# A two-layer decoder trunk: down projections whose sums are collected by adding transfers, with five pairs per group by seven block products

## The chip, the cores and the metric

The kernel runs on one core of one Trainium2 chip. The time is the device time of one execution in microseconds (us). A core has a matrix engine (TensorE, here PE, with its weight loads as PEld), a vector engine (VectorE, DVE), a scalar engine (ScalarE, ACT), a general engine (GpSimd, POOL) and a sync engine (SyncE, SP), which here only issues transfers. Each engine works through its own list in order and waits on semaphores of the others. Transfers (DMA) run beside them and raise a semaphore when they land.

## The reference, cut to what matters

The model has two layers over 256 tokens of width 2048. Layer A is a gated spatial mixer, layer B a latent attention; both have an attention into 256 memory tokens beside them, and each is followed by a gated ConvFFN:

```python
def conv_ffn(h, w_up, cw, cb, w_down):          # D_FF = 5632, width 3
    a = h @ w_up                                 # 2048 -> 11264
    ap = jnp.pad(a, ((0, 0), (CONV_W - 1, 0), (0, 0)))
    c = sum(ap[:, k:k + S] * cw[k] for k in range(CONV_W)) + cb
    gate, val = c[..., :D_FF], c[..., D_FF:]
    return (jax.nn.silu(gate) * val) @ w_down    # 5632 -> 2048

x = x + conv_ffn(rmsnorm(x, g_ffn[l]), w_ffn_up[l], conv_w[l], conv_b[l], w_ffn_down[l])
```

Everything is float32. The change is in the last product, `@ w_down`.

## The kernel before

Every float32 weight tile is split into a high part (`whi`, an ACT copy) and a low part (`wlo`, a DVE subtraction, raw minus high), and each product is made of three matmuls: high by high, high by low, low by high. A weight tile thus goes through four steps: SP issues its load into a `raw` buffer (four buffers of 128x1024, 512 KB each), ACT makes `whi`, DVE makes `wlo` (four buffers of each), TensorE multiplies.

`ffn` works through the hidden width in three groups of 4, 4 and 3 times 512 (`FF_GROUPS`). For each group the up projection is computed by `gemm_fm`, the convolution by `conv` on DVE and ACT, and the result is kept in `h`, sixteen blocks of 128 hidden units for the groups of four. Then this group's part of the down projection follows. For the first two groups of each layer this is `gemm_seven`, the function that the change rewrites; there are four such calls in the kernel, called groups below. The third group of a layer goes through `gemm_fm` or `gemm_tm`.

`gemm_seven` treats `h` as eight pairs of blocks and the output as two halves of 1024 columns, so it has sixteen steps, half 0 and then half 1, pairs 0 to 7 in each. A step is the product of a 2x2 arrangement: two blocks of tokens, two blocks of hidden units (a pair), two blocks of 512 output columns. A plain pair takes eight block products of three matmuls each, 24 matmuls, added up in four banks (`out`). The pairs in `SEVEN` take seven block products, 21 matmuls, as in Strassen's scheme in a form with few sums: three of the seven use differences of weight blocks (`differences`, on DVE, into `gate` buffers, split like any weight), four use sums of blocks of `h` (`block_sums`, computed in the up projection). Four results go to banks of their own (`side`) and are combined at the end of a half (`combined`). A seven pair thus needs four `whi` and four `wlo`, a plain pair two of each.

The steps are a software pipeline. In iteration i the program issues the first differences of step i + 2, then the split parts of step i + 1 (`prepare`), then the second differences of step i + 2, and then the matmuls of step i (`products`). The order on PE, ACT, DVE and SP is held as written (`manual_schedule`); elsewhere a scheduler sets it. A pair's raw data is loaded where it is first asked for (`load`, from `differences` or `prepare`).

The results of a half are added into `total` (layer A) or `xt` (layer B) in on-chip memory: `collected` adds the four banks, `combined` writes or adds the block products' sums, all of it by DVE (`add`, line 297). The small sums are spread over the following steps, three per step.

Of the kernel before, what the change touches and what calls it, by code (L numbers as in the profile page):

```python
# [8 lines left out]
F32 = mybir.dt.float32  # L9
# [7 lines left out]
P = 128  # L17
# [17 lines left out]
WARM = 7  # L35
SEVEN = (3, 5)

# [65 lines left out]
class Kernel:  # L103
# [189 lines left out]

    def gemm_seven(self, dn, n, h, s7, total, fresh, pool):
        nc = self.nc
        sub = lambda o, a, b: nc.vector.tensor_tensor(o, a, b, ALU.subtract)
        add = lambda o, a, b: nc.vector.tensor_tensor(o, a, b, ALU.add)
        ET = mybir.EngineType
        steps = [(half, m) for half in range(2) for m in range(n)]
        src = lambda i, c: self.rows(dn, (2 * steps[i][0] + c) * 512, 512)(2 * steps[i][1], 2)  # L300
        seven = lambda i: i < len(steps) and steps[i][1] in s7
        raws, early, ready, later = {}, {}, {}, []
        out, side = {}, {}

        def load(i):
            raws[i] = [self.raw_load(src(i, c)) for c in range(2)]

        def differences(i, part):
            if part == 0:
                load(i)  # L310
                early[i] = [self.tmp(pool, [P, 4, S], "gate", 2).rearrange("p a s -> p (a s)") for _ in range(2)]
            (b11, b21), (b12, b22) = ((raw[:, :512], raw[:, 512:]) for raw in raws[i])
            (t1, t2), (t3, t4) = ((t[:, :512], t[:, 512:]) for t in early[i])
            if part == 0:
                sub(t1, b12, b11)
                sub(t3, b22, b12)
            else:
                sub(t2, b22, t1)
                sub(t4, b21, t2)

        def prepare(i):
            if i not in raws:
                load(i)
            one, two = raws.pop(i)
            if seven(i):
                ta, tb = early.pop(i)
                ready[i] = [self.weight_parts(w) for w in (one, two[:, 512:], ta, tb)]
            else:
                ready[i] = [self.weight_parts(w) for w in (one, two)]

# [3 lines left out]
        def products(i):  # L334
            half, m = steps[i]
            parts = ready.pop(i)
            pick = lambda w, j: (w[0][:, j, :], w[1][:, j, :])
            if m == 0:
                for key in ((0, 0), (0, 1), (1, 0), (1, 1)):
                    out[key] = self.psum()  # L340
            if not seven(i):
                for c in range(2):
                    for tb in range(2):
                        for j in range(2):
                            first, last = m + j == 0, m == n - 1 and j == 1
                            self.three(out[tb, c], block(2 * m + j, tb), pick(parts[c], j), first, last)
                return
            first, last = m == min(s7), m == max(s7)
# [4 lines left out]
            one, b22, ta, tb = parts  # L353
            self.three(side[1], block(2 * m, 0), pick(one, 0), first, last)
            self.three(out[0, 0], block(2 * m + 1, 0), pick(one, 1))
            self.three(out[0, 1], s[3], pick(b22, 0))
            self.three(side[5], s[0], pick(ta, 0), first, last)
            self.three(side[6], s[1], pick(ta, 1), first, last)
            self.three(side[7], s[2], pick(tb, 0), first, last)
            self.three(out[1, 0], block(2 * m + 1, 1), pick(tb, 1))  # L360
            if last:
                later.extend(combined(half, dict(side)))
# [5 lines left out]
        def combined(half, p):  # L368
# [23 lines left out]
            if not fresh:  # L392
                todo += [lambda k=k, at=at: add(to[at], to[at], t[k]) for k, at in ((1, (0, 0)), (5, (0, 1)), (7, (1, 0)), (0, (1, 1)))]
            return todo

        def collected(half, accs):
            return [lambda at=at, acc=acc: add(place(half, *at), place(half, *at), acc) for at, acc in accs.items()]

        with self.tc.manual_schedule(engines={ET.PE, ET.Activation, ET.DVE, ET.SP}):
            prepare(0)  # L400
            for i in range(len(steps)):
                if seven(i + 2):
                    differences(i + 2, 0)
# [8 lines left out]
                if steps[i][1] == n - 1:  # L412
                    later.extend(collected(steps[i][0], dict(out)))
            for f in later:
                f()
# [74 lines left out]
    def masks(self):  # L490
        nc, cp = self.nc, self.cp
        self.ident = cp.tile([P, P], F32, name="ident")
# [29 lines left out]
    def rope_tables(self, la):  # L522
# [30 lines left out]
        nc.vector.tensor_tensor(k, k, k, ALU.mult)  # L553
        self.cosT = cp.tile([P, S], F32, name="cosT")
        self.sinT = cp.tile([P, S], F32, name="sinT")
        nc.vector.tensor_scalar(self.cosT, k, -2.0, 1.0, ALU.mult, ALU.add)
# [226 lines left out]
    def next_operand(self, j, gain):  # L783
# [6 lines left out]
        self.square_add(self.ssum, x, j == 0, self.cp)  # L790

# [13 lines left out]

    def ffn(self, l, sums, total, fresh, after=None, hooks={}, tokens=None):
        nc, t = self.nc, self.t
# [4 lines left out]
        with self.tc.tile_pool(name=self.uid("ff"), bufs=1) as fp:  # L812
            g0 = 0
            for part, ng in enumerate(FF_GROUPS):
# [41 lines left out]
                if not last:  # L856
                    self.gemm_seven(dn, 2 * ng, h, s7, total, fresh and part == 0, fp)
                    g0 += ng
                    continue
# [104 lines left out]
    def layer_b(self):  # L964
# [9 lines left out]
        with tc.tile_pool(name="lb", bufs=1) as lb:  # L974
# [8 lines left out]
            def latent(name):  # L983
# [3 lines left out]
                def evict(b, acc):  # L987
                    self.scaled(lat[:, b : b + 2, :], acc, rb)
                    self.square_add(sums, lat[:, b : b + 2, :], b == 0, self.cp)

# [182 lines left out]
    def first_ffn(self):  # L1173
        nc, tc = self.nc, self.tc
        with tc.tile_pool(name="sums", bufs=1) as sp:
# [4 lines left out]
            def turn(a, i):  # L1180
                small[a, i] = self.tmp(sp, [P, 1024], "s7" if a == 0 else "square", len(SEVEN) if a == 0 else 2)
                src = total[:, a, 1024 * i : 1024 * (i + 1)]
# [21 lines left out]
            }  # L1204
            self.ffn(0, sp, total, True, after=lambda j: self.next_operand(j, None), hooks=hooks)

    def run(self):
# [10 lines left out]
        with tc.tile_pool(name="fin", bufs=1) as fin, tc.tile_pool(name="sums", bufs=1) as sums_pool:  # L1218
# [11 lines left out]
            def gains():  # L1230
                gb.append(slot()[:, :D])
                nc.sync.dma_start(out=gb[0], in_=t["g_final"].rearrange("(o d) -> o d", o=1).to_broadcast([P, D]))

# [123 lines left out]
```

## Time and profile before

| | |
|---|---|
| median of 3 runs | 2037.37 us (2033.04 to 2039.13) |
| the profiled execution | 2035.25 us, span 2033.5 us |
| PE, DVE, ACT, POOL busy | 2020.3, 1493.2, 1080.7, 95.1 us |
| granted TensorE clock | 0.999 |
| the first `gemm_seven`, 520.6 to 605.0 us | PE busy 83.64 of 84.4 us, DVE 69.35, ACT 43.00; DMA share 0.61 |
| the third, 1481 to 1570 us | PE busy 86.96 of 89 us; DMA share 0.60 |

In the profile, a group row reads: line, engine, operation, output tile and input tiles, shape and count, then the busy time and the mean duration in ns of one, then the idle time of the engine ahead of them and what ended it. The durations of matmuls are from start to end and overlap; TensorE's rate is read from the distance of two starts. A waits row reads: who waited for whom, then the total in us, how often, and the longest. Transfers show the median time from issue to landing. Tile names stand without their numbers, so that `raw7` may appear as `raw`.

### The profile page before, as it was taken

The numbers are of one execution on the slowest core, as the hardware profiler recorded it, in microseconds if no ns is written. First come the engines' busy times: TensorE is split into PE (matmuls) and PEld (weight loads), VectorE is DVE, ScalarE is ACT, GpSimd is POOL, SyncE is SP. The second block draws the span as 40 slices with busy tenths as digits, with TensorE's granted clock in tenths as the row PEclk, the third lists the DMA queues.
The fourth block names the chain that finished last, engine by engine and source line by source line (L and its number), as shares of the span: only waits on it lengthen the run. The fifth ranks groups of instructions, "written<-read, shape, count | busy, mean of one in ns | idle before, by whom it ended". The sixth has DMA issues, their size and how long they took to land.

```text
span 2033.5 us, 37724 instructions
## 1 busy us (share of the span) xinstructions
PE 2020.3 (99%) x15394; PEld 1923.9 (95%) x15394; DVE 1493.2 (73%) x2064; ACT 1080.7 (53%) x1424; POOL 95.1 (5%) x131
## 2 busy tenths in 40 slices
PE   9999999999999999999999999999999999999998
PEld 8989999999889998899999999999988999889997
DVE  6866667767776777877789886777678667786675
ACT  6754644555545555445546674455544555544543
POOL 0000013000000000000052002200000000000000
PEclk9999999999999999999999999999999999999999
DMA  8675855666566665688665565578756666566654
GB/s 312 186 236 176 199 179 186 206 190 192 185 213 190 195 196 180 213 214 214 190 195 185 172 151 166 192 209 214 222 186 199 195 201 188 183 204 195 199 185 154
DMA packets 254013, 398.86 MB, mean 196 GB/s; under 512 B 65040, under 2 KB 71824, under 8 KB 253712
## 3 DMA queue, kind: packets, MB, share of 16 engines
q1 hardware_dynamic: 253264, 395.80, 64.7%
q8 instruction: 120, 1.97, 0.4%
q10 hardware_dynamic: 576, 0.66, 0.1%
q14 instruction: 53, 0.43, 0.1%
HBM read 388.01 MB, written 2.10 MB: 192 GB/s over the span
## 4 chain that ended last, share of the span: by engine, by line
PE 94%; DVE 3%; DMA 2%; issue 1%; ACT 1%; ACTq 0%; POOLq 0%; POOL 0%; DVEq 0%
PE ps L180 23%; PE ps L181 23%; PE ps L183 23%; PE ps L291 4%; PE ps L292 4%; PE ps L290 4%; PE ps L211 3%; PE ps L212 3%; PE ps L213 3%; DMA raw<-in_w_ffn_down 1%; DVE wlo L270 1%; DVE c L828 0%; ACT whi L269 0%; PE ps L714 0%; PE ps L767 0%
## 5 line engine op out<-in xcount | busy, mean ns | idle before, releaser
L144 DVE TENSOR_TENSOR wlo<-raw,whi 128x1024 fp32r<-128x1024 f32 (+1 forms) x544 | 664.3, 1238 | 396.2 <-issue 254.0
L143 ACT ACTIVATE whi<-raw 128x1024 fp32r<-128x1024 f32 (+1 forms) x544 | 569.4, 1054 | 574.1 <-PE ps L181 435.6
L180 PE MATMUL ps<-xhl,whi 128*128 128x256 f32 x3264 | 750.6, 276 | 0.0
L181 PE MATMUL ps<-xhl,whi 128*128 128x256 f32 x3264 | 750.2, 276 | 0.0
L180 PEld LDWEIGHTS ps<-xhl,whi 128*128 128x128 f32 x3264 | 612.6, 188 | 0.2
L181 PEld LDWEIGHTS ps<-xhl,whi 128*128 128x128 f32 x3264 | 612.6, 188 | 0.2
L183 PE MATMUL ps<-xhl,wlo 128*128 128x256 f32 x3264 | 403.2, 276 | 0.0
L183 PEld LDWEIGHTS ps<-xhl,wlo 128*128 128x128 f32 x3264 | 385.2, 188 | 0.0
L269 ACT ACTIVATE whi<-raw 128x1024 fp32r<-128x1024 f32 (+1 forms) x128 | 126.0, 1004 | 113.8 <-DMA raw<-in_w_ffn_down 45.8
L270 DVE TENSOR_TENSOR wlo<-raw,whi 128x1024 fp32r<-128x1024 f32 (+1 forms) x128 | 144.8, 1155 | 48.3 <-ACT whi L269 22.2
L291 PE MATMUL ps<-wlo,h 128*128 128x512 f32 x432 | 168.7, 391 | 2.5 <-DVE wlo L270 2.5
L290 PE MATMUL ps<-whi,h 128*128 128x512 f32 x432 | 168.4, 390 | 1.3 <-ACT whi L269 1.3
L292 PE MATMUL ps<-whi,h 128*128 128x512 f32 x432 | 168.2, 389 | 0.0
L828 DVE SCALAR_TENSOR_TENSOR c<-a,cT,c 128x255 f32<-128x255 f32 (+1 forms) x352 | 145.9, 477 | 0.0
L825 ACT ACTIVATE c<-a,cT 128x256 f32<-128x256 f32 x176 | 91.6, 591 | 77.4 <-DVE a L419 77.4
L180 PE MATMUL ps<-mainhl,whi 128*128 128x256 f32 x512 | 118.5, 278 | 0.0
L181 PE MATMUL ps<-mainhl,whi 128*128 128x256 f32 x512 | 118.0, 277 | 0.0
L291 PEld LDWEIGHTS ps<-wlo,h 128*128 128x128 f32 x432 | 81.1, 188 | 21.2 <-DVE wlo L270 4.4
L290 PEld LDWEIGHTS ps<-whi,h 128*128 128x128 f32 x432 | 81.1, 188 | 18.6 <-ACT whi L269 1.9
L292 PEld LDWEIGHTS ps<-whi,h 128*128 128x128 f32 x432 | 81.1, 188 | 16.8
L180 PEld LDWEIGHTS ps<-mainhl,whi 128*128 128x128 f32 x512 | 96.0, 188 | 0.1
L181 PEld LDWEIGHTS ps<-mainhl,whi 128*128 128x128 f32 x512 | 96.0, 188 | 0.1
(325 smaller groups left out, 2389.6 us busy)
## 6 DMA issues: line engine op xcount, KB each, us to landing
raw<-in_w_ffn_up SPq DMA_DIRECT2D x352, 512.0 KB, 4.2
raw<-in_w_ffn_down SPq DMA_DIRECT2D x176, 512.0 KB, 4.8
raw<-in_w_out SPq DMA_DIRECT2D x64, 512.0 KB, 4.9
raw<-in_w_in_a SPq DMA_DIRECT2D x56, 512.0 KB, 4.5
raw<-in_w_mem_kv SPq DMA_DIRECT2D x31, 512.0 KB, 5.3
raw<-in_w_in_b SPq DMA_DIRECT2D x16, 512.0 KB, 3.9
raw<-in_w_uq SPq DMA_DIRECT2D x12, 384.0 KB, 3.4
raw<-in_w_kv_a SPq DMA_DIRECT2D x8, 512.0 KB, 3.7
```

The source lines that it names most:

```text
L143: nc.scalar.activation(hi[:, :n], raw[:, :n], AF.Copy)
L144: nc.vector.tensor_tensor(lo[:, :n], raw[:, :n], hi[:, :n].bitcast(F32), ALU.subtract)
L180: mm(acc, wh, x[:, :S], start=first, stop=False)
L181: mm(acc, wh, x[:, S:], start=False, stop=False)
L183: mm(acc, wl, x[:, :S], start=False, stop=last)
L269: nc.scalar.activation(hi, raw, AF.Copy)
L270: nc.vector.tensor_tensor(lo, raw, hi.bitcast(F32), ALU.subtract)
L290: mm(acc, xh, wh, start=start, stop=False)
L291: mm(acc, xh, wl, start=False, stop=False)
L292: mm(acc, xl, wh, start=False, stop=stop)
L825: nc.scalar.activation(c[:, i, :], a[:, i, :], AF.Identity, scale=w(2), bias=w(3))
L828: nc.vector.scalar_tensor_tensor(o, a[:, i, : S - 2 + j], w(j), o, ALU.mult, ALU.add)
```

## The change

- The pairs by seven block products are now 4 and 6 in half 0 and 2, 4 and 6 in half 1, where they were 3 and 5 in both. In half 0 the pairs run in the order 0, 1, 2, 4, 3, 6, 5, 7 (`PASSES`). By position in the sixteen steps, counted from 0, the seven pairs stand at 3, 5, 10, 12 and 14; before they stood at 3, 5, 11 and 13.
- A seven pair's raw weights, 1 MB, go to a tile of their own, `raw7`, with one buffer, in three transfers: a row of 128x1024 and two of 128x512. Plain pairs keep the four `raw` buffers. Room for `raw7` is made by moving constants to other pools, and in layer B it is the second half of the gain vector's tile.
- All loads are asked for in the order of the steps, two steps ahead.
- The first two differences are now one instruction of 128x1024.
- Sums that were added to `total` by DVE are now added by transfers on POOL's queue with an adding operation (`collect`). A bank's result is first copied by ACT to a `c` buffer (three buffers, shared with the convolution), since the transfer starts from there. The first group of layer A still writes the block products' sums straight to `total`.
- Four instead of three of the small steps run per step.

```diff
-SEVEN = (3, 5)
+SEVEN = (2, 4, 6)
+PASSES = (((0, 1, 2, 4, 3, 6, 5, 7), (4, 6)), ((0, 1, 2, 3, 4, 5, 6, 7), (2, 4, 6)))
...
         def load(i):
-            raws[i] = [self.raw_load(src(i, c)) for c in range(2)]
+            half, m = steps[i]
+            if not seven(i):
+                blocks[i] = [self.raw_load(src(i, c)) for c in range(2)]
+                return
+            raw = blocks[i] = raw7()
+            row = lambda j: self.rows(dn, half * 1024, 1024)(2 * m + j, 1).rearrange("p k (c n) -> p (k c) n", c=2)
+            nc.sync.dma_start(out=raw[:, 0:2, :], in_=row(0))
+            for c in range(2):
+                nc.sync.dma_start(out=raw[:, 3 - c, :], in_=row(1)[:, c, :])
 
         def differences(i, part):
+            raw = blocks[i]
             if part == 0:
-                load(i)
...
+                sub(early[i][0], raw[:, 1:3, :], raw[:, 0:2, :])
+                return
+            t13, t24 = early[i]
+            sub(t24[:, 0, :], raw[:, 2, :], t13[:, 0, :])
+            sub(t24[:, 1, :], raw[:, 3, :], t24[:, 0, :])
...
             if not fresh:
-                todo += [lambda k=k, at=at: add(to[at], to[at], t[k]) for k, at in ((1, (0, 0)), (5, (0, 1)), (7, (1, 0)), (0, (1, 1)))]
+                todo += [lambda k=k, at=at: collect(to[at], t[k]) for k, at in ((1, (0, 0)), (5, (0, 1)), (7, (1, 0)), (0, (1, 1)))]
             return todo
 
+        def collect(to, x):
+            nc.gpsimd.dma_start(out=to, in_=x, accum_op=ALU.add)
+
         def collected(half, accs):
-            return [lambda at=at, acc=acc: add(place(half, *at), place(half, *at), acc) for at, acc in accs.items()]
+            def one(at, acc):
+                c = self.tmp(pool, [P, 2, S], "c", 3).rearrange("p a s -> p (a s)")
+                nc.scalar.activation(c, acc, AF.Copy)
+                collect(place(half, *at), c)
+
+            return [lambda at=at, acc=acc: one(at, acc) for at, acc in accs.items()]
 
         with self.tc.manual_schedule(engines={ET.PE, ET.Activation, ET.DVE, ET.SP}):
+            load(0)
+            load(1)
             prepare(0)
             for i in range(len(steps)):
+                if i + 2 < len(steps):
+                    load(i + 2)
                 if seven(i + 2):
                     differences(i + 2, 0)
                 if i + 1 < len(steps):
                     prepare(i + 1)
                 if seven(i + 2):
                     differences(i + 2, 1)
-                now, later[:] = later[:3], later[3:]
+                now, later[:] = later[:4], later[4:]
                 products(i)
...
-            self.ffn(0, sp, total, True, after=lambda j: self.next_operand(j, None), hooks=hooks)
+            self.ffn(0, sp, total, True, lambda: self.tmp(sp, [P, 4, 512], "raw7", 1), after=lambda j: self.next_operand(j, None), hooks=hooks)
...
-            self.ffn(1, sums_pool, xt, False, hooks=turns, tokens=tokens)
+            self.ffn(1, sums_pool, xt, False, lambda: gb[0][:, D:].rearrange("p (a n) -> p a n", a=4), hooks=turns, tokens=tokens)
```

Three places where the order of instructions changes. First SP's queue, at the loads of the first `gemm_seven`; a row gives the buffer's number, the weight matrix, the shape and the semaphores waited for. Before, from position 2 and 3 on (the seven pair's loads, 757 and 758, stand ahead of position 2's, 761 and 762):

```order
L262 DMA raw_757_6086<-in_w_ffn_down 128x2x512 [waits DMAHW0_49,DVE_49]
L262 DMA raw_758_6088<-in_w_ffn_down 128x2x512 [waits DMAHW1_49,DVE_49]
L262 DMA raw_761_6094<-in_w_ffn_down 128x2x512 [waits DMAHW2_49,DVE_49]
L262 DMA raw_762_6096<-in_w_ffn_down 128x2x512 [waits DMAHW3_49,DVE_49]
L262 DMA raw_775_6172<-in_w_ffn_down 128x2x512 [waits DMAHW6_49,DVE_49]
L262 DMA raw_776_6174<-in_w_ffn_down 128x2x512 [waits DMAHW7_49,DVE_49,Activation_49]
L262 DMA raw_779_6180<-in_w_ffn_down 128x2x512 [waits DMAHW4_49,DVE_49]
L262 DMA raw_780_6182<-in_w_ffn_down 128x2x512 [waits DMAHW5_49,DVE_49]
```

Now the same place:

```order
L263 DMA raw_751_6058<-in_w_ffn_down 128x2x512 [waits DMAHW0_49,DVE_49]
L263 DMA raw_752_6060<-in_w_ffn_down 128x2x512 [waits DMAHW1_49,DVE_49]
L316 DMA raw7_761_6098<-in_w_ffn_down 128x1024 [waits PE_49,Pool_49]
L318 DMA raw7_761_6098<-in_w_ffn_down 128x512 x2
L263 DMA raw_768_6139<-in_w_ffn_down 128x2x512 [waits DMAHW2_49,DVE_49]
L263 DMA raw_769_6141<-in_w_ffn_down 128x2x512 [waits DMAHW3_49,DVE_49]
L316 DMA raw7_778_6183<-in_w_ffn_down 128x1024 [waits DMAHW6_49,DMAHW0_49,DMAHW7_49,DVE_49,Activation_49]
L318 DMA raw7_778_6183<-in_w_ffn_down 128x512 [waits DMAHW4_49]
L318 DMA raw7_778_6183<-in_w_ffn_down 128x512 [waits DMAHW5_49]
L263 DMA raw_789_6225<-in_w_ffn_down 128x2x512
L263 DMA raw_790_6227<-in_w_ffn_down 128x2x512
```

Position 4's load (768, 769) has moved ahead of position 5's (778), and position 5's now waits for DVE's and ACT's reads of position 3 out of the one `raw7` buffer; position 6's load (789, 790) stands right behind it.

Second DVE, at the same place. Now:

```order
L297 TENSOR_TENSOR gate_763_6103<-raw7_761_6098,gate_763_6103 128x512 [waits DMAHW7_49,DVE_49]
L271 TENSOR_TENSOR wlo_771_6144<-raw7_761_6098,whi_770_6143 128x512 [waits PE_49]
L271 TENSOR_TENSOR wlo_773_6148<-raw7_761_6098,whi_772_6147 128x1024 [waits PE_49]
L271 TENSOR_TENSOR wlo_775_6152<-gate_762_6102,whi_774_6151 128x1024 [waits Activation_49]
L271 TENSOR_TENSOR wlo_777_6156<-gate_763_6103,whi_776_6155 128x1024 [waits Activation_49]
L297 TENSOR_TENSOR gate_779_6187<-raw7_778_6183 128x1024 [waits DMAHW5_49,DMAHW3_49,DVE_49]
L271 TENSOR_TENSOR wlo_782_6191<-raw_768_6139,whi_781_6190 128x1024 [waits DMAHW1_49,Activation_49]
L271 TENSOR_TENSOR wlo_784_6195<-raw_769_6141,whi_783_6194 128x1024 [waits DMAHW2_49,Activation_49]
L297 TENSOR_TENSOR gate_780_6188<-raw7_778_6183,gate_779_6187 128x512 [waits DVE_49]
L297 TENSOR_TENSOR gate_780_6188<-raw7_778_6183,gate_780_6188 128x512 [waits DMAHW4_49,DVE_49]
L271 TENSOR_TENSOR wlo_792_6230<-raw7_778_6183,whi_791_6229 128x512 [waits Activation_49]
L271 TENSOR_TENSOR wlo_794_6234<-raw7_778_6183,whi_793_6233 128x1024 [waits Activation_49]
```

Position 5's first difference (`gate_779`) stands ahead of position 4's low parts (`wlo_782`, `wlo_784`), as it did before; but its load is now the one that starts after `wlo_773`, the last read of position 3's `raw7`.

Third ACT, where half 0's results are collected during position 8. Now:

```order
L270 ACTIVATE whi_823_6391<-raw_813_6346 128x1024 [waits DMAHW5_49,DVE_49,PE_49]
L408 ACTIVATE c_829_6425<-ps_757_6070 128x512
L408 ACTIVATE c_830_6428<-ps_758_6071 128x512
L408 ACTIVATE c_831_6431<-ps_759_6072 128x512
L408 ACTIVATE c_832_6434<-ps_760_6073 128x512 [waits DMASW0_49,Activation_49]
L270 ACTIVATE whi_835_6441<-raw7_818_6380 128x512 [waits DMAHW6_49,DVE_49,PE_49]
L270 ACTIVATE whi_837_6445<-raw7_818_6380 128x1024 [waits DMAHW0_49,DMAHW7_49,DVE_49,PE_49]
```

The four copies are new on ACT (before, ACT went from one `whi` to the next here); the fourth waits for `DMASW0`, the landing of the first copy's transfer on POOL's queue, and position 10's `whi` stand behind it.

More of the change, by code (lines that the diff above doesn't have):

```diff
@@ L298, in gemm_seven @@
         ET = mybir.EngineType
-        steps = [(half, m) for half in range(2) for m in range(n)]
+        steps = [(half, m) for half, (order, _) in enumerate(passes) for m in order]
         src = lambda i, c: self.rows(dn, (2 * steps[i][0] + c) * 512, 512)(2 * steps[i][1], 2)
-        seven = lambda i: i < len(steps) and steps[i][1] in s7
-        raws, early, ready, later = {}, {}, {}, []
+        seven = lambda i: i < len(steps) and steps[i][1] in passes[steps[i][0]][1]
+        begins = [passes[half][0][0] == m for half, m in steps]
@@ L303, in gemm_seven @@
+        ends = [passes[half][0][-1] == m for half, m in steps]
+        heavy = [[i for i in range(len(steps)) if steps[i][0] == half and seven(i)] for half in range(len(passes))]
+        blocks, early, ready, later = {}, {}, {}, []
         out, side = {}, {}
         def load(i):
-            raws[i] = [self.raw_load(src(i, c)) for c in range(2)]
+            half, m = steps[i]
[7 more added lines that the diff above has]
+                nc.sync.dma_start(out=raw[:, 3 - c, :], in_=row(1)[:, c, :])
@@ L308, in differences @@
         def differences(i, part):
+            raw = blocks[i]
             if part == 0:
-                load(i)
[L311 to L319, printed above, removed]
+                early[i] = [self.tmp(pool, [P, 4, S], "gate", 2).rearrange("p (a b) s -> p a (b s)", a=2) for _ in range(2)]
+                sub(early[i][0], raw[:, 1:3, :], raw[:, 0:2, :])
+                return
@@ L321, in prepare @@
+            t13, t24 = early[i]
+            sub(t24[:, 0, :], raw[:, 2, :], t13[:, 0, :])
+            sub(t24[:, 1, :], raw[:, 3, :], t24[:, 0, :])
         def prepare(i):
-            if i not in raws:
-                load(i)
-            one, two = raws.pop(i)
+            raws = blocks.pop(i)
             if seven(i):
[L326 to L329, printed above, removed]
+                flat = lambda x: x.rearrange("p a s -> p (a s)")
+                raws = [raws[:, 0, :], flat(raws[:, 2:4, :])] + [flat(t) for t in early.pop(i)]
@@ L344, in products @@
                         for j in range(2):
-                            first, last = m + j == 0, m == n - 1 and j == 1
+                            first, last = begins[i] and j == 0, ends[i] and j == 1
                             self.three(out[tb, c], block(2 * m + j, tb), pick(parts[c], j), first, last)
                 return
-            first, last = m == min(s7), m == max(s7)
+            first, last = i == heavy[half][0], i == heavy[half][-1]
             if first:
@@ L352, in products @@
             s = [(s7[m][:, 0, j, :], s7[m][:, 1, j, :]) for j in range(4)]
[L353 to L360, printed above, removed]
+            b11, b2, t13, t24 = parts
+            self.three(side[1], block(2 * m, 0), pick(b11, 0), first, last)
+            self.three(out[0, 0], block(2 * m + 1, 0), pick(b2, 1))
+            self.three(out[0, 1], s[3], pick(b2, 0))
+            self.three(side[5], s[0], pick(t13, 0), first, last)
+            self.three(side[7], s[2], pick(t13, 1), first, last)
+            self.three(side[6], s[1], pick(t24, 0), first, last)
+            self.three(out[1, 0], block(2 * m + 1, 1), pick(t24, 1))
             if last:
@@ L803, in w_out, with ffn @@
             group(g)
-    def ffn(self, l, sums, total, fresh, after=None, hooks={}, tokens=None):
+    def ffn(self, l, sums, total, fresh, raw7, after=None, hooks={}, tokens=None):
         nc, t = self.nc, self.t
@@ L856, in ffn @@
                 if not last:
-                    self.gemm_seven(dn, 2 * ng, h, s7, total, fresh and part == 0, fp)
+                    self.gemm_seven(dn, PASSES, h, s7, total, fresh and part == 0, fp, raw7)
                     g0 += ng
@@ L1180, in turn @@
             def turn(a, i):
[L1181 removed]
+                if a == 0:
+                    small[a, i] = self.tmp(sp, [P, 1024], "s7", len(SEVEN))
+                elif i == 0:
+                    both = self.tmp(sp, [P, 2, 1024], "raw7", 1)
+                    small[1, 0], small[1, 1] = both[:, 0, :], both[:, 1, :]
                 src = total[:, a, 1024 * i : 1024 * (i + 1)]
```

21 lines of the change are left out of this document (11 added, 10 removed).

## The prediction

> **What bounds the kernel now.** I read the page first: busy shares and the chain that ended last.
>
> ```profile
> span 2033.5 us, 37724 instructions
> PE 2020.3 (99%) x15394; PEld 1923.9 (95%) x15394; DVE 1493.2 (73%) x2064; ACT 1080.7 (53%) x1424; POOL 95.1 (5%) x131
> PE ps L180 23%; PE ps L181 23%; PE ps L183 23%; PE ps L291 4%; PE ps L292 4%; PE ps L290 4%; PE ps L211 3%; PE ps L212 3%; PE ps L213 3%; DMA raw<-in_w_ffn_down 1%; DVE wlo L270 1%; DVE c L828 0%; ACT whi L269 0%; PE ps L714 0%; PE ps L767 0%
> ```
>
> TensorE sets the end; the stages to change are lines 290 to 292. Next, what TensorE waited for there, from the waits of PE, and then the chain through the start of a down projection, where such a wait arises (start, duration, piece).
>
> ```profile
> PE ps L291 <- DVE wlo L270: 2.5, 4, 0.8
> PE ps L290 <- ACT whi L269: 1.3, 1, 1.3
> ```
> ```profile
> 534.05 1.15 DVE wlo L270
> 535.21 5.35 DMA raw<-in_w_ffn_down
> 540.66 1.07 ACT whi L269
> 541.76 1.23 DVE wlo L270
> 543.04 0.50 PE ps L291
> 543.76 0.23 PE ps L290
> ...
> 544.44 0.23 PE ps L290
> ```
>
> The same chain of the whole span has such a load at the other three groups too:
>
> ```profile
> 794.79 4.95 DMA raw<-in_w_ffn_down
> ...
> 1496.48 6.99 DMA raw<-in_w_ffn_down
> ...
> 1757.95 5.28 DMA raw<-in_w_ffn_down
> ```
>
> Only 2.5 + 1.3 = 3.8 us of TensorE waiting belongs to these stages, so nothing large can be won. But the chain shows how thin the cover is: a `raw` buffer is read for the last time, only then is the next load issued, 5 to 7 us later it lands, is split by ACT and DVE, and TensorE has run dry. This happens once in each of the four groups, at the fifth pair. Three matmuls take 544.44 - 543.76 = 0.68 us, so one is 0.227; a plain pair of 24 takes 5.45, a seven pair of 21 takes 4.77, both together 10.2 us.
>
> **The matmuls.** A seven pair is one computed by seven block products instead of eight. There are 20 of them instead of 16 (five per group), and each new one saves one block product of three matmuls: 4 x 3 x 0.227 = **2.7 us off**. Pair 4's old wait goes as well, since its load now stands ahead of the next seven pair's: **3.8 us off**.
>
> **The raw buffer.** A seven pair's 1 MB now goes to `raw7`, which exists once, instead of to two of the four `raw` buffers. Durations by shape, over the whole run:
>
> ```profile
> L270 DVE TENSOR_TENSOR wlo<-raw,whi 128x1024 fp32r<-128x1024 f32 x112 | 135.2, 1222 | 48.3 <-ACT whi L269 22.2 <-issue 18.5 <-PE ps L183 6.2
> L269 ACT ACTIVATE whi<-gate 128x1024 fp32r<-128x1024 f32 x32 | 34.0, 1062 | 56.4 <-PE ps L292 52.6 <-DVE wlo L270 3.8
> L296 DVE TENSOR_TENSOR gate<-raw,gate 128x512 f32<-128x512 f32 x32 | 22.0, 688 | 0.4
> L270 DVE TENSOR_TENSOR wlo<-raw,whi 128x512 fp32r<-128x512 f32 x16 | 10.9, 684 | 0.0
> L269 ACT ACTIVATE whi<-raw 128x512 fp32r<-128x512 f32 x16 | 10.0, 625 | 9.4 <-PE ps L292 6.2 <-ACT whi L269 3.2
> L284 DVE TENSOR_TENSOR s<-c,s 128x512 fp32r<-128x512 f32 x8 | 5.6, 694 | 5.8 <-ACT s L283 5.8
> L281 DVE TENSOR_TENSOR c<-hv 128x128 f32<-128x128 f32 x16 | 3.9, 283 | 0.0
> L375 ACT ACTIVATE a<-ps 128x512 f32<-128x512 f32 x6 | 3.5, 580 | 0.0
> ```
> ```profile
> 533.96 1.83 DVE L270 TENSOR_TENSOR wlo<-raw,whi 128x1024 fp32r<-128x1024 f32 x2
> ```
>
> By the order on DVE, what lies between the landing of one seven pair and the last read of its buffer is: the first difference (128x1024, 1.22), the two low parts of the pair before it (2 x 1.22), two differences of 512 (2 x 0.69), and the low parts of its own two raw pieces (0.68 + 1.22): 6.9 us, and since a 1.22 and a 0.68 end in 1.83 in the row above, each start overlaps by 0.08: **6.5 us**. Then the next load may start. Behind that load wait DVE's next difference, behind this on the same engine the plain pair's low parts (already landed), and behind them TensorE.
>
> How long does 1 MB take? Rows for it:
>
> ```profile
> 541.98 2.53 ACT L269 ACTIVATE whi<-raw 128x1024 fp32r<-128x1024 f32 x3 [0.26 <-DMA raw<-in_w_ffn_down]
> ```
> ```profile
> raw<-in_w_ffn_down SPq DMA_DIRECT2D x176, 512.0 KB, 4.8
> xt<-slot SPq DMA_DIRECT2D x16, 128.0 KB, 5.6
> turned<-square SPq DMA_DIRECT2D x16, 64.0 KB, 6.1
> slot<-in_g_final SPq DMA_DIRECT2D x1, 1024.0 KB, 4.9
> out_y<-xt SPq DMA_DIRECT2D x3, 256.0 KB, 2.9
> ...
> turned<-in_w_sp SPq DMA_DIRECT2D x1, 768.0 KB, 9.4
> ```
>
> In the chain the first half of a pair lands 5.35, 4.95, 6.99 and 5.28 us after its issue (mean 5.6), the second half 541.98 - 540.66 = 1.3 later: 6.9 for 1 MB. The gain vector's 1 MB took 4.9, the lower bound. In the new order SP issues the following 1 MB right behind; shared fully it would add 2 x 1.3: 9.6, the upper bound. I take 7.3, close to the pair, which is the same tensor on the same queue.
>
> Three loads per group must wait for the one buffer (positions counted from 0):
> - Position 5 after 3. Before, the last raw read of position 3 ended at 533.96 + 1.83 = 535.8. The sums of the new sixth pair now stand ahead of it on DVE (4 x 0.28 + 0.69 = 1.8): 537.6. Plus 7.3, plus difference and low part (2.3): 547.2. TensorE wants it at 543.04 less its wait, about 542.0: **5.2** (2.8 to 7.5).
> - Position 12 after 10. The buffer's last reads need a free `whi`, which comes when TensorE ends position 8 (the 52.6 us in the row of L269 are such waits): 1.06 + 1.22 later the load starts, 7.3 + 2.3 later the low part of position 11 is there: 11.9 against 10.4 (10.2 and one matmul): **1.5** (0 to 3.8).
> - Position 14 after 12, now in a closed ring: 6.5 + 7.3 = 13.8 against 10.2: **3.6** (1.2 to 5.9).
>
> Sum 10.3 per group, **41 us** (16 to 69).
>
> **The adding transfers.** 32 results go from a matmul bank to `c` by an ACT copy (0.58 each, L375) and from there by a POOL-queue transfer; 24 more, in the three groups that are not the first, leave `a` and `hv`. DVE loses 56 adds, which is worth nothing, since DVE is not the bound. But `c` has three buffers and each half has four results: the fourth copy waits on ACT until the first transfer has landed, X after its issue, and behind it on ACT stand the next `whi`. No row shows an adding transfer. The nearest are 2.9 (256 KB to HBM), 5.6 and 6.1 (small pieces moved inside the on-chip memory); the slowest of all is 9.4. I take X = 5.6, since it too stays on the chip, and keep 2.9 and 9.4 as the ends.
> In mid-group the first copy ends 0.58 into position 8, and the fourth at X + 1.16; then 0.63 + 1.06 + 1.22 until the buffer of position 10 is free: X + 4.1 instead of 5.45 + 2.3 = 7.75. X - 3.7 = 1.9, four times: 7.6. At a group's end the fourth `whi` of the next projection, wanted after 5.45 + 1.8 = 7.25 (48 and 16 matmuls of half the length), stands behind the fourth copy. In the first group it comes at X + 0.58 + 0.58 + 1.06 = 7.8: 0.6 late. In the three groups that add to earlier totals the first copy's transfer also waits for the block product's on the same quarter, issued 0.58 into the last pair: that lands at X + 0.58 - 5.45 = 0.7, the copy's at 6.3, `whi` at 6.3 + 0.58 + 1.06 = 8.0: 0.8 late, three times. Together **11 us** (0, or with 9.4: 4 x 5.7 + 4.4 + 3 x 8.4 = 52).
>
> [...]
>
> **Sum.** -2.7 - 3.8 + 41 + 11 = +46 us on the profiled execution's 2035.25 (span 2033.5 and 1.75 around it): 2081. The median of the runs shown, 2037.37, is 2 above it: **2083**. The added sums of pairs 2 and 4 in each up projection lie in DVE's idle time there (busy 73% by the page; uncovered, 4 x 1.8 = 7 us) and the moved constants cost nothing.
>
> **Rivals.**
> 1. Quick loads: 1 MB in 4.9 as the gain vector, and transfers in 2.9. 16 + 0 - 6.5: +9.5, 2047 on the median. For it: rows of 4 KB in one piece. Against it: four measured pairs. 0.13. [...]
> 2. Slow adding transfers, X = 9.4: 41 + 52 - 6.5 = +86, 2124. For it: small pieces already take 6.1, and these queue behind one another on POOL. Against it: each is only 256 KB in rows of 2 KB. 0.14.
> 3. Faster: the two old waits go and no new one comes. This needs 1 MB within 10.2 - 6.5 = 3.7 us in the ring, and within 542.0 - 537.6 - 2.3 = 2.1 at position 5. Then 6.5 us come off: 2031. For it: plain pairs are now loaded a step earlier, so the queue is emptier when the buffer comes free. Against it: even 512 KB has a median of 4.8. 0.03.
> 4. No change: 1 MB in 3.7, so that the ring costs nothing and position 5 costs 4 x 1.6 = 6.4, which takes the 6.5 back: 2037. The same row speaks against it. 0.05.
>
> My forecast has 0.65. This measurement tells about 0.3% (6 us) from no change. Slower 0.90 (a part of rival 1 falls within 6 us), same 0.07, faster 0.03. The range 2045 to 2135 reaches from quick loads to slow transfers; the forecast's own is 2055 to 2115.
>
> **What would show it.** Right: DVE's difference line (now 297) waits for DMA tens of us in total; TensorE's line 292 waits for `wlo` at the pair ahead of a seven pair, three times per group, and the chain there reads load, difference, low part, matmul; the fourth ACT copy (line 408) waits for a POOL transfer. Wrong: if the 1 MB lands under 5 us, or the difference finds its data waiting, the 41 falls; if line 408 never waits, the 11 falls.

## The result, and the profile after

| | before | after |
|---|---|---|
| median | 2035.8 us | 2101.74 us (2099.7 to 2109.52) |
| ratio, 95% interval | | 1.033 (1.0299 to 1.0362) |
| the profiled execution, its span | 2035.25, 2033.5 us | 2102.6, 2100.9 us |
| granted TensorE clock | 0.999 | 0.987 |

The change makes the kernel 66 us slower. The page of the kernel after, with the rows that answer to those of before (the chain by engine, the matmuls on a low part):

```profile
span 2100.9 us, 37918 instructions
PE 2044.0 (97%) x15382; PEld 1936.2 (92%) x15382; DVE 1482.1 (71%) x2032; ACT 1109.8 (53%) x1468; POOL 144.2 (7%) x187
PE 86%; DMA 6%; DVE 4%; issue 2%; SPq 1%; ACT 1%; DVEq 0%; POOLq 0%; POOL 0%; ACTq 0%
L292 PE MATMUL ps<-wlo,h 128*128 128x512 f32 x412 | 171.2, 416 | 47.1 <-DVE wlo L271 47.1
```

And its waits (who for whom, total us, times, longest):

```profile
PE ps L292 <- DVE wlo L271: 47.1, 21, 4.9
DVE gate L297 <- DMA slot<-in_w_ffn_down: 38.4, 9, 8.8
DVE gate L297 <- DMA raw<-in_w_ffn_down: 34.7, 9, 9.3
ACT c L408 <- DMA xt<-c: 20.9, 4, 6.5
ACT c L408 <- DMA total<-c: 14.3, 4, 6.1
```

(`slot` is the place of the one buffer in layer B.) Two things are read here. TensorE now waits 47.1 us for low parts, where 3.8 us were waited in these stages before: 43 us more. And it is busy *longer*, 2044.0 against 2020.3 us, with 12 matmuls less (2.7 us): its matmuls took 26 us more. 43 + 26 - 2.7 = 67, which is the difference of the spans, 2100.9 - 2033.5. By the distances of starts, 20 of the 26 us are matmuls that came more slowly; most of the rest is stall that the page counts as busy, since it models where a matmul ends.

The chain of the kernel after at the first such wait, at position 4 of the first group:

```profile
537.35 0.68 DVE gate L297
538.04 1.75 DVE wlo L271 x2
...
540.72 5.67 DMA raw<-in_w_ffn_down
...
546.51 0.06 DVE gate L297
...
547.65 1.23 DVE wlo L271
...
548.92 0.79 PE ps L292
549.72 0.43 PE ps L293
550.14 0.43 PE ps L291
```

It reads as the prediction had it: the last reads of the one buffer (538.04), the load of position 5, DVE's difference of it, and only then the low part of position 4, for which TensorE stands. The last two rows show the rest: a matmul every 0.43 us, where one took 0.227. The clock in the same stretch (column PEclk, third from the end; busy time and count per engine before it):

```profile
540.00:544.00 4.00, 4.00 (x18) 3.13 (x18) 2.05 (x2) 1.64 (x2) 0.00 (x0) 1.00 0.69 187
544.00:549.00 5.00, 0.31 (x3) 0.08 (x1) 2.49 (x3) 1.69 (x2) 0.00 (x0) 0.86 0.80 270
549.00:553.00 4.00, 4.00 (x10) 3.13 (x11) 3.96 (x5) 0.00 (x0) 0.00 (x0) 0.50 0.57 176
```

TensorE's granted clock falls from 1.00 to 0.50 towards the end of the stall (1.00 from 547.0 to 547.6, 0.50 from 547.7 to 548.7) and stays there for microseconds after the data has come (0.50 from 548.9 to 554.4, 1.00 from 554.5 on). In the trace of after there are eleven such stretches behind stalls, each 3.4 or 6.8 us long. So 47 us of waiting bring some 20 us of slow matmuls with them.

### The profile page after: what moved, and what is told of

It is laid out like the page before. It is cut to its first block, busy times and chain, and to the rows that moved or that the text cites. A ratio compares the mean times of both kernels' runs of the same rounds, so it can differ in the third digit from the quotient of the medians.

```text
span 2100.9 us, 37918 instructions
## 1 busy us (share of the span) xinstructions
PE 2044.0 (97%) x15382; PEld 1936.2 (92%) x15382; DVE 1482.1 (71%) x2032; ACT 1109.8 (53%) x1468; POOL 144.2 (7%) x187
## 4 chain that ended last, share of the span: by engine, by line
PE 86%; DMA 6%; DVE 4%; issue 2%; SPq 1%; ACT 1%; DVEq 0%; POOLq 0%; POOL 0%; ACTq 0%
PE ps L181 23%; PE ps L182 23%; PE ps L184 22%; DMA slot<-in_w_ffn_down 3%; DMA raw<-in_w_ffn_down 3%; PE ps L212 3%; PE ps L213 3%; PE ps L214 3%; PE ps L292 3%; PE ps L293 2%; DVE wlo L271 2%; PE ps L291 2%; DVE gate L297 1%; DVE c L846 0%; ACT whi L270 0%
## 5 line engine op out<-in xcount | busy, mean ns | idle before, releaser
L145 DVE TENSOR_TENSOR wlo<-raw,whi 128x1024 fp32r<-128x1024 f32 (+1 forms) x544 | 665.2, 1238 | 403.5 <-issue 233.2
L144 ACT ACTIVATE whi<-raw 128x1024 fp32r<-128x1024 f32 (+1 forms) x544 | 570.4, 1056 | 530.5 <-PE ps L182 355.6
L292 PE MATMUL ps<-wlo,h 128*128 128x512 f32 x412 | 171.2, 416 | 47.1 <-DVE wlo L271 47.1
L270 ACT ACTIVATE whi<-raw 128x1024 fp32r<-128x1024 f32 (+1 forms) x108 | 109.8, 1020 | 87.3 <-PE ps L293 29.3
L271 DVE TENSOR_TENSOR wlo<-raw,whi 128x1024 fp32r<-128x1024 f32 (+1 forms) x108 | 123.1, 1171 | 30.7 <-issue 18.1
```

The lines of the kernel that those rows point to most:

```text
L144: nc.scalar.activation(hi[:, :n], raw[:, :n], AF.Copy)
L145: nc.vector.tensor_tensor(lo[:, :n], raw[:, :n], hi[:, :n].bitcast(F32), ALU.subtract)
L270: nc.scalar.activation(hi, raw, AF.Copy)
L271: nc.vector.tensor_tensor(lo, raw, hi.bitcast(F32), ALU.subtract)
L292: mm(acc, xh, wl, start=False, stop=False)
```

## The experiments

The theory at the start: the one buffer makes a seven pair's load late, and DVE, which works in order, stands before that load with the plain pair's low parts queued behind (position 5's difference ahead of position 4's low parts), so that TensorE stops too; the adding transfers add some 11 us. The rival: the transfers are the main cost, by the bandwidth they take. Each run is compared with the kernel before on its own chip, which had medians of 2034.88, 2034.71 and 2033.48 us for the three sets of four below. Totals of waits are the page's; the length of a single wait is the distance of two matmul starts less the 0.227 us of one matmul, 0.2 us more than the page gives it.

**DVE's order.** The changed kernel, with a seven pair's first differences behind the plain pair's low parts:

```diff
-                if seven(i + 2):
-                    differences(i + 2, 0)
                 if i + 1 < len(steps):
                     prepare(i + 1)
                 if seven(i + 2):
+                    differences(i + 2, 0)
                     differences(i + 2, 1)
```

> Edit: the first differences of a seven pair are put behind the low parts of the plain pair before it, instead of ahead of them; nothing else. Theory A (the one raw7 buffer's load is waited for on DVE, and the plain pair's finished data stands behind that wait): the waits at positions 4, 9, 11 and 13 (about 37 of the 47 us of TensorE waiting) nearly vanish, and with them most of the half-clock time that follows them; position 3's 7 us of waiting stay: 2040 to 2055. Theory B (the transfers with adding slow all weight loads, and DVE's order matters little, since the seven pair itself then waits): 2080 or more. Theory C (the added block sums and the longer work at the start of a group): no change at positions 9 to 13, 2085 to 2100.

Measured: 2044.76 us, ratio 1.0047 (1.0032 to 1.0063). Two moved lines give back 57 of the 66 us. TensorE's waits, and DVE at the place shown above:

```profile
PE ps L292 <- DVE wlo L271: 5.8, 13, 1.5
PE ps L291 <- ACT whi L270: 3.4, 3, 1.9
```
```profile
540.12 2.35 DVE L271 TENSOR_TENSOR wlo<-raw,whi 128x1024 fp32r<-128x1024 f32 x2
545.01 1.22 DVE L297 TENSOR_TENSOR gate<-raw 128x1024 f32<-128x1024 f32 x1 [2.53 <-DMA raw<-in_w_ffn_down]
```

DVE still waits 2.53 us for the same load, from the same one buffer, but position 4's low parts are now ahead of the wait. The late loads are still there; what turned them into TensorE's time was the work queued behind them.

**The adding transfers.** The changed kernel with the sums added by DVE, as before:

```diff
-            nc.gpsimd.dma_start(out=to, in_=x, accum_op=ALU.add)
+            add(to, to, x)
...
-                c = self.tmp(pool, [P, 2, S], "c", 3).rearrange("p a s -> p (a s)")
-                nc.scalar.activation(c, acc, AF.Copy)
-                collect(place(half, *at), c)
+                collect(place(half, *at), acc)
```

> Edit: the sums are again added by DVE, straight from the banks; no adding transfers and no copies by ACT; raw7, the five pairs and all the rest as changed. Theory A: the waits at position 4 (19 us in four groups) and those of the ring at positions 11 and 13 stay; position 9's (three groups, 10 us and 7 us of half clock) go, since they come with 13 us loads among four adding transfers: 2075 to 2090. Theory B: 2035 to 2050. By the term of the prediction for the transfers, 11 us and its share of half clock, 2085.

Measured: 2090.8 us, ratio 1.0283 (1.0262 to 1.0305): the transfers are worth 2101.7 - 2090.8 = 11 us in the changed kernel (with four executions of each, good to some 7 us). The rival, that they are the main cost, falls. The waits at position 9 (2.7 to 3.6 us in groups 2 to 4) are gone; those at positions 3, 4, 11 and, smaller, 13 stay, 37.1 us in all.

**The buffer.** The changed kernel with seven pairs loaded into the four `raw` buffers again, still in the order of the steps, two ahead (the first two differences are two instructions again):

```diff
-            raw = blocks[i] = raw7()
-            row = lambda j: self.rows(dn, half * 1024, 1024)(2 * m + j, 1).rearrange("p k (c n) -> p (k c) n", c=2)
-            nc.sync.dma_start(out=raw[:, 0:2, :], in_=row(0))
-            for c in range(2):
-                nc.sync.dma_start(out=raw[:, 3 - c, :], in_=row(1)[:, c, :])
+            blocks[i] = [self.raw_load(src(i, c)) for c in range(2)]
```

> Edit: seven pairs are loaded into two of the four raw buffers again, with the four small differences of before; five pairs per group, the loads two steps ahead in the order of the steps, and the adding transfers stay. Theory A: waits at positions 4, 11 and 13 go, what stays is what the transfers do to loads near position 8 and to ACT: 2035 to 2055. Theory B: 2080 or more. Theory C: 2085 or more.

Measured: 2086.69 us, ratio 1.0258 (1.024 to 1.0276). A miss: four buffers gave back 15 us, not most of it. SP and DVE of this kernel at position 5's load:

```profile
539.94 0.37 SPq L263 DMA_DIRECT2D raw<-in_w_ffn_down  x1
```
```profile
545.38 0.69 DVE L297 TENSOR_TENSOR gate<-raw,raw 128x512 f32<-128x512 f32 x1 [0.21 <-DMA raw<-in_w_ffn_down]
546.60 2.35 DVE L271 TENSOR_TENSOR wlo<-raw,whi 128x1024 fp32r<-128x1024 f32 x2
```

Position 5's load starts at 539.94, no earlier than with the one buffer (539.86, from the trace of after). Four buffers are two pairs, and where loads go in the order of the steps, step i + 2 gets the buffers of step i: the same ring from 3 to 5, from 10 to 12 and to 14. For TensorE the two are not equal. In the first group the difference waits only 0.21 us for this load and TensorE not at all at position 4, since it had stood at position 2 already. Over the four groups the waits at positions 4, 11 and 13 are 18 us, where the change has 31; in place of the 7 us at position 3 there are 10 us at position 2, where the ring from 1 to 3 and the late sums (below) meet, which no run separates. In the kernel before, the corresponding load left nine microseconds earlier, since a seven pair's load was asked for ahead of the plain pair's and took the place of the plain pair 2, while the plain pair 4, which needs no differences, got the late place of pair 3:

```profile
530.53 0.37 SPq L262 DMA_DIRECT2D raw<-in_w_ffn_down  x1
```
```profile
539.60 0.69 DVE L296 TENSOR_TENSOR gate<-raw,raw 128x512 f32<-128x512 f32 x1
540.21 0.69 DVE L296 TENSOR_TENSOR gate<-raw 128x512 f32<-128x512 f32 x1
541.76 1.22 DVE L270 TENSOR_TENSOR wlo<-raw,whi 128x1024 fp32r<-128x1024 f32 x1 [0.87 <-ACT whi L269]
```

There the difference doesn't wait for its load. So "the number of buffers" names only a part of the cause; the other is which step hands its buffers to which (with the old order of the loads, below, 3 us are left of those 18, though other waits there may cover some).

**The clock.** The kernel before, with chains of needless DVE products ahead of the low parts of positions 7 and 15, of eight lengths:

```diff
+            for _ in range(doses.get(i, 0)):
+                nc.vector.tensor_tensor(self.idle, self.idle, self.idle, ALU.mult)
             one, two = raws.pop(i)
```

> Edit: the kernel before, with chains of 19 to 40 added DVE products on a small tile of zeros ahead of the split parts of positions 7 and 15 in each of the four groups: eight stalls of TensorE of growing length. If the half clock seen in the changed kernel is a consequence of a stall's length, stalls under some 3 us cost their own length alone, and longer ones are followed by 3.4 or 6.8 us at a clock of 0.5, which costs another 1.7 to 3.4 us. If it comes from something else in the change, no window at 0.5 follows any stall here.

Measured: 2112.57 us, a single execution, with stalls of 4.6 to 11.9 us. Around the first one:

```profile
552.00:558.00 6.00, 6.00 (x28) 4.99 (x27) 5.66 (x12) 3.67 (x4) 0.00 (x0) 1.00 0.59 196
558.00:563.00 5.00, 0.77 (x4) 0.31 (x3) 4.72 (x11) 1.06 (x1) 0.00 (x0) 0.77 0.00 0
563.00:567.00 4.00, 4.00 (x10) 3.13 (x11) 3.96 (x6) 0.00 (x0) 0.00 (x0) 0.50 0.59 160
```

No transfer was moving there (DMA share 0.00), and the clock fell all the same: 0.77 over these 5 us, 0.50 over the four behind them. All eight stalls were followed by half clock. With the stalls of all fourteen profiled executions of this study (the distance of two matmul starts less 0.06 us; over 0.7 us, those closer than 2 us taken as one; the slow stretch at the very end of every execution left out):

| stall of TensorE | stalls | followed by half clock | length at half clock |
|---|---|---|---|
| 0.7 to 1.9 us | 53 | 0 | |
| 1.9 to 3.5 us | 43 | 22 | 3.4, in two cases 6.8 us |
| 3.5 to 7 us | 29 | 29 | 3.4 or 6.8 us |
| 7.2 to 11.9 us | 4 | 4 | 10.2 or 13.7 us |

The lengths count from where the clock falls, so they hold a part of the stall. Half of the stalls between 1.9 and 3.5 us were followed by half clock, in the trace of after three under 3 us among them (1.96, 2.51 and 2.83 us). So the expectation that a stall under some 3 us costs its own length alone does not hold.

Within these 1.9 to 3.5 us the length does not tell which. In the trace of after, stalls of 1.96, 2.51, 2.83, 3.23 and 3.48 us were followed by half clock, and those of 2.00, 2.23 and 3.37 us were not. What sets the two kinds apart was not shown.

**Both repairs, and the loads' order.** The second set: the moved differences with DVE's adds; the four buffers with the loads asked for as before the change (a seven pair's two ahead and first, a plain pair's one ahead); the four buffers in the order of the steps with the moved differences; and the old loads with DVE's adds. The edits are those shown, and for the old loads:

```diff
         def differences(i, part):
+            if part == 0:
+                load(i)
...
         def prepare(i):
+            if i not in blocks:
+                load(i)
...
-            load(0)
-            load(1)
...
-                if i + 2 < len(steps):
-                    load(i + 2)
```

> Both repairs together in the changed kernel: a seven pair's differences stand behind the low parts of the plain pair ahead of it on DVE, and the sums are added by DVE again, with no adding transfer. The one buffer and five seven pairs per group stay. If order and transfers are the two causes, their gains add: the order alone left 2044.8, of which the transfers' stalls (positions 9, 10, 13, 14) were some 10 us, so 2031 to 2038, TensorE's wait on DVE's low parts under 4 us. Rival: DVE, which gets 56 sums of 0.69 = 38 us back, is then late itself and the gains do not add: 2040 to 2055.

Measured: 2033.24 us, ratio 0.9992 (0.9984 to 1.0001). The gains add: with DVE's order mended and the transfers gone, one buffer and five seven pairs take no longer than the kernel before. The transfers cost 11 us here too (2044.8 to 2033.2).

> The four raw buffers back, loads in step order two pairs ahead (this alone: 2086.7), and the differences behind the plain pair's low parts on DVE. If what hurts is that DVE waits for a seven pair's load with landed work queued behind the wait, the order mends it here too: 2036 to 2052. If with four buffers it is another cause (a plain pair's load late because a seven pair's fills the buffers): 2065 or more.

Measured: 2038.5 us, ratio 1.002 (1.0008 to 1.0033), inside its range. The order mends this ring as well: 2086.7 to 2038.5.

> The four raw buffers back, and the loads issued as in the kernel before: a seven pair's load two pairs ahead and in front of the plain pair's, which is issued one pair ahead. Five seven pairs per group, the differences' place on DVE and the adding transfers stay as in the changed kernel. The run with the four buffers and loads in step order gave 2086.7. If the order of the loads against that of the differences is the cause: 2038 to 2055, and the stalls at positions 2, 4, 11 and 13 fall to 1 us or less, those at position 9 (adding transfers) stay. Rival: three seven pairs in six of a half are too dense for DVE, whatever the loads' order: 2070 or more, stalls stay at positions 11 and 13.

Measured: 2087.88 us, ratio 1.0261 (1.0245 to 1.0277). A miss for the theory as it stood. The waits at positions 4, 11 and 13 did fall to about 1 us, as expected, but those at position 2 were 3.3 to 3.9 us, and positions 9 and 10 together took 2.4 us in the first group and 6.6 to 7.0 in the others. Position 10 of the second group, in this kernel's chain:

```profile
846.41 6.92 DMA total<-c
...
853.41 0.06 ACT c L405
...
853.90 1.06 ACT whi L270
...
854.98 1.84 DVE wlo L271 x2
```

That is the wait predicted for the transfers: the fourth `c` copy on ACT waits for an adding transfer, and position 10's `whi` stand behind it.

> As the run with the old loads, and with the sums added by DVE again, so that of the whole change only the fifth seven pair per group is left (with the moved constants and pair sums). Theory: 12 matmuls less, 2.7 us, and no new wait: 2028 to 2036. Rival, five pairs are too dense for DVE: 2060 or more.

Measured: 2059.55 us, ratio 1.012 (1.0106 to 1.0134). Without the transfers 28 us go, but the expectation is missed by 24 us and the rival's figure (2060 or more) is all but met: with all that bears on the waits as before but the pairs, five seven pairs per group cost 25 us. Some 20 us of it are the wait at position 2, 3.3 to 3.6 us in every group with 1.5 to 1.7 us of slow matmuls behind. DVE ahead of this place, in the changed kernel, where it is the wait at position 3:

```profile
530.85 0.68 DVE L859 TENSOR_TENSOR hv<-gate,c 128x512 f32<-128x512 f32 x1
531.57 0.49 DVE L282 TENSOR_TENSOR c<-hv 128x128 f32<-128x128 f32 x2
...
533.05 1.27 DVE L846 SCALAR_TENSOR_TENSOR c<-a,cT,c 128x255 f32<-128x255 f32 x3
534.23 0.69 DVE L285 TENSOR_TENSOR s<-c,s 128x512 fp32r<-128x512 f32 x1
...
535.35 0.69 DVE L859 TENSOR_TENSOR hv<-gate,c 128x512 f32<-128x512 f32 x1
```

And the last two `hv` of the up projection in the kernel before:

```profile
527.35 1.28 DVE L841 TENSOR_TENSOR hv<-gate,c 128x512 f32<-128x512 f32 x2
```

The last `hv` ends at 536.0 instead of 528.6. Between the last two stand the sums of pair 6 (lines 282 and 285), which also take one of the three `c` buffers that the convolution of the last blocks needs (read from the program, not tested by itself). Pair 6 is nearly the last to come out of the up projection; before, no sum was formed after pair 5. All that DVE and ACT do at the start of the down projection moves back.

**The late sums.** The third set tests this by other pairs at the same positions:

```diff
-SEVEN = (2, 4, 6)
-PASSES = (((0, 1, 2, 4, 3, 6, 5, 7), (4, 6)), ((0, 1, 2, 3, 4, 5, 6, 7), (2, 4, 6)))
+SEVEN = (1, 3, 5)
+PASSES = (((0, 1, 2, 3, 4, 5, 6, 7), (3, 5)), ((0, 2, 1, 4, 3, 6, 5, 7), (1, 3, 5)))
```

> The changed kernel with other pairs by seven products: pairs 3 and 5 in the first half and 1, 3 and 5 in the second, at the same positions 3, 5, 10, 12 and 14 (before: pairs 4, 6 and 2, 4, 6). What moves is only which pairs' sums are formed in the up projection: pair 6's, which came among the last results of the up projection, go, and pair 5's come instead. If those late sums are what holds DVE and ACT up at the start of each down projection, the waits at position 3 (1.6 to 2.1 us) go and those at position 4 (4.5 to 5.1) fall to 3.4 or less, with the half clock after some of them: 2070 to 2088. If the buffer alone is the cause there, nothing moves: 2097 to 2106.

Measured: 2082.55 us, ratio 1.0245 (1.0229 to 1.0261): 19 us less than the change. The waits at position 3 are gone, as expected; those at position 4 are still 2.2 to 5.5 us, more than expected, so they belong to the ring.

> The kernel that had 2059.6 (four raw buffers and loads as before the change, DVE adds, five seven pairs), with pair 5's sums in place of pair 6's, positions unchanged. Its stalls were 3.3 to 3.6 us at position 2 in every group, with 1.5 to 1.7 of half clock behind. If the late sums cause them, all four go: about 20 us less, 2035 to 2043. If the fifth pair as such is too much for DVE: 2052 or more.

Measured: 2039.52 us, ratio 1.0031 (1.002 to 1.0041). The four waits at position 2 go, and with them 18 us by the ratios, 20 by the medians. TensorE's waits for low parts in the two kernels, with pair 6 and with pair 5 instead:

```profile
PE ps L292 <- DVE wlo L271: 17.7, 11, 3.4
```
```profile
PE ps L292 <- DVE wlo L271: 6.1, 10, 0.8
```

The fifth pair as such is not too much for DVE; where its sums are formed was.

**All repairs.** Two kernels were made to beat the one before. The first has five seven pairs per group, four buffers with loads in the order of the steps, DVE's adds, pair 5's sums and the differences behind the low parts:

> All repairs together, with five seven pairs per group: four raw buffers, DVE adds, pair 5's sums in place of pair 6's, and the differences behind the plain pair's low parts. No wait on DVE's low parts is left in the middle of a group; what stays is 0.8 us at the end of each (the next projection's first low parts stand behind the sums of the seven pair at position 14): -2.7 - 3.8 + 3.4 = -3 against before, 2030 to 2034. Rival: the seven pair's load, now behind the plain pair's, is late in its turn: 2036 or more.

Measured: 2028.07 us (2027.62 to 2029.5), ratio 0.9973 (0.9962 to 0.9983): faster than both kernels, by 5.4 us than the one before, and below the range that was expected. The page has no wait left on the low parts (the last number of the second row). The 0.8 us at the ends, which I had taken for a wait, are eight matmuls of the next projection, 0.115 apart, that run among those of the last pair (the first of them below):

```profile
PE 2016.0 (100%) x15382; PEld 1922.1 (95%) x15382; DVE 1514.5 (75%) x2108; ACT 1089.7 (54%) x1436; POOL 95.1 (5%) x131
L292 PE MATMUL ps<-wlo,h 128*128 128x512 f32 x412 | 160.3, 389 | 0.0
```
```profile
601.87 0.28 PE L181 MATMUL ps<-xhl,whi 128*128 128x256 f32 x1
```

The second is the kernel before with nothing but the moved differences (its load moves with them):

> The kernel before with one edit: a seven pair's load and first differences behind the plain pair's load and low parts, instead of in front. Four seven pairs per group. If the order on DVE was what its old waits at position 4 came from (3.8 us in all), they go and nothing comes: 2029 to 2033. If the seven pair's load, issued later, is late in turn: 2036 or more.

Measured: 2030.66 us, ratio 0.9986 (0.9977 to 0.9994), in its range: the old waits at position 4 go too. Between the two, without any wait, stand the 12 matmuls: 2030.66 - 2028.07 = 2.6 us, good to some 0.7.

From the kernel before to the changed one, one thing after another, by the ratios (times 2034 us; they do not add independently, since a wait that is there already can cover the next):

| added | run | ratio | us added |
|---|---|---|---|
| five seven pairs, with pair 5's sums | old loads, DVE's adds, early sums | 1.0031 | 6 |
| pair 6's sums in their place | old loads, DVE's adds | 1.0120 | 18 |
| the one buffer, loads in the order of the steps | the change with DVE's adds | 1.0283 | 33 |
| the adding transfers | the change | 1.033 | 10 |

## Why the prediction was right, and where it was not

The direction, the main place and the two main causes were right; the time was 2102 instead of 2083, inside both ranges. The sum was +46 and the spans differ by +67. By the prediction's steps:

- **The matmuls, 2.7 us off: right.** 2.6 us between two kernels that wait for nothing in these stages.
- **Pair 4's old wait, 3.8 us off: in effect not.** It went only to come back larger in the same place. With pair 5's sums and the old loads, waits of 0.5 to 1.0 us at positions 4, 11 and 13 remain, 6.1 us in all; it takes DVE's order to lose them.
- **The buffer, 41 us: near in its size, half right in its cause.** Position 5's load waits for position 3's last reads, and TensorE waits 4.5 to 5.1 us at position 4 (5.2 predicted). In the kernel with DVE's adds, where the transfers don't blur it, the waits at positions 4, 11 and 13 are on the average 4.1, 3.2 and 0.9 us (5.2, 1.5 and 3.6 predicted): 8.2 per group for 10.3, 33 us in all. But I put it down to one buffer instead of four. Four in the order of the steps hand over to the same steps; the changed order of the loads was in the lists that I quoted, and I did not follow which buffers each would get.
- **The adding transfers, 11 us: right in its size, by DVE's adds (11 us), too short in its term X, and in part at another place.** That the size came out is partly luck: the same transfers cost 28 us in the kernel with the old loads (2087.9 to 2059.6). X was taken as 5.6. The medians from issue to landing in the kernel after are (size, us):

```profile
total<-c POOLq DMA_DIRECT2D x16, 256.0 KB, 5.9
xt<-c POOLq DMA_DIRECT2D x16, 256.0 KB, 7.6
xt<-a POOLq DMA_DIRECT2D x8, 256.0 KB, 9.3
total<-hv POOLq DMA_DIRECT2D x4, 256.0 KB, 8.9
```

  The waits fell mostly at position 9, not at 11, because there the load for position 10 was caught among four of them. The chain at this place in the second group, the issue and the load:

```profile
838.97 0.50 SPq L318
...
839.51 13.40 DMA raw<-in_w_ffn_down
```

  Of the rows that I had for X, the small pieces moved inside the on-chip memory (5.6 and 6.1) came nearer to these landings than the 256 KB to HBM (2.9).
- **The step that failed: a wait was priced at its own length.** The sum had no term for the slowed clock, and that is the largest thing that it missed: 26 us of longer busy time behind stalls of 2 to 5 us, some 20 of it slow matmuls. In the trace of before no stall was followed by it (four of 0.9 to 1.6 us, two of them close together), so the rows that I went by could not show it.
- **The late sums were mis-sized.** "The sums of the new sixth pair now stand ahead of it on DVE" counted their 1.8 us of DVE time per group, once, in the load of position 5. They took 18 to 20 us in all (with the old loads and DVE's adds; 19 in the changed kernel), as they also hold a `c` buffer, push the last `hv` back by 7 us and make TensorE wait at position 3 (1.6 to 2.1 us per group, 7 in all), where nothing was foreseen.

In the trace of after: 52 us of waits were predicted (41 + 11), 47.1 came, 7 of them the unforeseen ones at position 3. So the foreseen waits were 12 too high, and 7 + 26 were missing: 46 - 12 + 7 + 26 = 67. That the forecast lay within 1% owes something to these two errors having opposite signs.

The signs named in advance were there: line 297 waits 38.4 + 34.7 us for its data, line 292 waits for `wlo` ahead of seven pairs, the chain reads load, difference, low part, matmul, and line 408's copies wait 20.9 + 14.3 us for transfers in eight halves.

What stays open: how much of the 33 us of the third row of the table is due to the single buffer as such, how much to the order of the loads and how much to their new split into three; with DVE's order mended, one buffer cost some 6 us more than four (2044.8 against 2038.5), with the transfers in both.

## What to carry to other kernels

On an engine that works in order, put work whose data has landed ahead of work that may have to wait, and look for the wait in what is queued behind it: two moved lines were worth 57 us here, more than any of the causes that made the load late. When buffers are few, ask which earlier step hands its buffer to this load, not only how many there are; changing the order of the loads changes that. And price a stall of TensorE with the slow microseconds behind it: here 3.4 us or more at half clock, a part of the stall among them, behind 22 of 43 stalls of 1.9 to 3.5 us and behind all 33 that were longer.

## What the runs showed of the hardware that was not expected

- A stall of TensorE of 3.5 us or more was followed by half clock in every one of 33 cases, one of 1.9 to 3.5 us in 22 of 43, a shorter one (over 0.7 us) in none of 53; the matmuls then came every 0.43 us for the rest of 3.4 or 6.8 us, up to 13.7 us behind the longest.
- An adding transfer of 256 KB between two places of the on-chip memory landed 5.9 to 9.3 us after its issue (medians), and the last part of a 1 MB load issued among four of them took 13.4 us, where such parts have medians of 6.1 and 6.3 in this kernel.
